# Keeping TensorE in source order through the scan stages of a hybrid decoder, and moving one pair of gate columns

## The chip, the cores and the metric

The kernel runs on one core of a Trainium2 chip. A core has TensorE (PE: matrix products, with its weight loads shown apart as PEld), VectorE (DVE), ScalarE (ACT), GpSimd (POOL) and SyncE (SP); each works through its own queue in order, and semaphores connect them. Transfers are issued from SP's and POOL's queues. The metric is the device time of one execution in microseconds (us).

## The reference, cut to what matters

One decoder layer is computed for 256 prompt positions and for 8 samples of 4 positions, 288 columns in all, so one weight pass serves both. The part that matters here is the mixer: two recurrent branches, merged by gates.

```python
xn = _rmsnorm(x, p['norm_mix'])
z, xbc, dt_raw, q, k, v, r, g_lr, gate_a, gate_b = _split(xn @ p['w_in'], IN_SIZES)
xbc, ssd_conv_new = _causal_dwconv(xbc, ssd_conv, p['ssd_conv_w'], p['ssd_conv_b'])
xs, Bm, Cm = _split(jax.nn.silu(xbc), ...)
y_ssd, ssd_state_new = _ssd_scan(xs_h, dt, A, Bm, Cm, ssd_state)      # 4 groups of 8 heads
u = (y_ssd + D * xs_h) * silu(z)
u = u * rsqrt(mean(u * u per group) + EPS) * ssd_norm
branch_a = u @ p['w_ssd_out']
...
o, gla_state_new = _gla_scan(qh, kh, vh, glog, gla_state)             # 4 heads
branch_b = (normalised o * silu(r)) @ p['w_gla_out']
merged = sigmoid(gate_a) * branch_a + sigmoid(gate_b) * branch_b
h = x + merged @ p['w_mix_out']
```

Cross-attention, the ConvFFN and the projections of the memory follow or precede it and are untouched.

## The kernel before, in words

**Main work.** Every large product is a projection (`proj_w`): two column tiles of 128 are accumulated over the depth. Weights come as `raw` tiles of 512 KB on SP's queue (3 buffers), and are split in two steps into a high part (`whi`, ACT, L103) and a low part (`wlo`, DVE, L105), 5 buffers each. Each half tile (two depth steps of 128) gives 12 matmuls of 288 columns: four each at L147 and L148 with the high part, four at L151 with the low part. After a half tile the generator yields. A projection of depth 16 has 8 half tiles, one of depth 4 has 2. When a projection is done, `cons` takes its two accumulators out of PSUM; accumulators have two tags with two buffers, used in turn.

**Scan work.** Between the half tiles stands the work of a scan: `ssd_scan` for the four SSD groups, then `gla_scan` for the four GLA heads. It is a generator too. In an SSD scan these PE steps come in order: products and transpositions of B, C and x (L755 to L763); the chunk's state products (L790 to L796); the products with the decay matrices (L837 to L841) and a transposition of the samples' x (L845); eight state updates (L907); the samples' product with their states (L886, with L889); the transposition back (L942); and in `finish` the sum of squares over the group (L972), which DVE and ACT prepare as a high and a low part (`sqh`, `sql`). The sample states are loaded on POOL's queue (L746, L734) and transposed on DVE (L900).

**Stages.** There are eight, n = 0 to 7. In stage n the scan of unit n runs as background, and `weave` pulls it so many steps for so many half tiles of main work (`N_BG[n]` steps in `N_MAIN[n]`). Main work is the projection of unit n+1, and, from n = 1, the output projection of unit n-1 (`project`) behind its first 16 half tiles. In stage 0, which has no such projection, the first half of the gate columns (`gate` with `gate_early`: 4 projections of 8 half tiles, called pairs of column tiles here) stands behind it instead. Their tanh is taken on ACT (L1231) and stored to DRAM on POOL's queue (L1233); it is read again in `project(3)` (`branch_a`), which runs in stage 4.

**Caches of the convolution.** The x, B and C columns pass through a short convolution on ACT, DVE and POOL (`conv_silu`); POOL copies the rows to keep into a cache tile (L638, L639). The cache is transposed on PE (L616). That step is put on a list (`late`), and `flush` runs it inside the next projection, behind its third half tile (its second in a projection of depth 4).

**Order.** The whole kernel is planned: `tc.block(schedule_with_timeline_sim=True)` simulates the engines and may issue an instruction ahead of an earlier one of the same engine that is not ready in the simulation. `tc.manual_schedule(engines=...)` takes the engines it names out of this: their instructions stay in the order in which the code gives them. It is used before for the first memory projection alone.

Of the kernel before, what the change touches and what calls it, by code (L numbers as in the profile page):

```python
# [27 lines left out]
O_Z, O_XBC, O_DT, O_Q, O_K, O_V, O_R, O_G, O_GA, O_GB = (  # L28
    0, 2048, 5120, 5152, 6176, 7200, 9248, 11296, 11312, 13360)
# [5 lines left out]
WB = 5  # L35
STOP = object()
LNEXP = "natural_log_exp_and_others"
N_MAIN = [64, 64, 48, 64, 64, 64, 64, 45]
N_BG = [60] * 4 + [44] * 3 + [47]


# [1 line left out]
def hybrid_step(ctx: ExitStack, tc: tile.TileContext, I: dict, O: list):  # L43
# [22 lines left out]
    def mm_tile():  # L66
        return ps.tile([P, 512], F32, tag="mm", bufs=3, name="mm")
# [96 lines left out]
    def proj(w, c0, ncol, X, nk, cons, row0=0):  # L164
        def load(k0, kn):
            return wload(rows_of(w, row0, k0, kn, c0, ncol))
        return proj_w(load, ncol, X, nk, cons)

    def run(*gens):
        for g in gens:  # L170
            for _ in g:
                pass

    def chain(*gens):
        for g in gens:
            yield from g

    def weave(main, bg, n_main, n_bg):

        done = 0  # L180
        for i, _ in enumerate(main):
            while done < (i + 1) * n_bg // n_main:
                w = next(bg, STOP)
                if w is STOP:
                    break
                done += 1 if w is None else w
        run(bg)

    def split_from(hi, lo, src, scale):
        S.activation(hi, src, ACT.Identity, scale=scale)  # L190
        V.scalar_tensor_tensor(lo, src, scale, hi, ALU.mult, ALU.subtract)

    def split(hi, lo, src):
        S.copy(hi, src)
        V.tensor_tensor(lo, src, hi, ALU.subtract)
# [10 lines left out]
    def bigf(name):  # L206
        return big.tile([P, KT, T], F32, tag="bigf", bufs=1, name=name)
# [15 lines left out]
    def rstd_from(pl, ssq, n, four=False):  # L223
        r = pl.tile([P, T], F32, tag="rstd", bufs=1, name="rstd")
        S.activation(r, ssq, ACT.Ln, scale=1.0 / n, bias=epsc[:, 1:2] if four else epsc[:, 0:1])
        S.activation(r, r, ACT.Exp, scale=-0.5)
        return r
# [351 lines left out]
    def b2r(name):  # L579
        return pa.tile([P, 512], F32R, tag="b2", bufs=10, name=name)  # L580
# [131 lines left out]
    def ssd_scan(g, xsT, sz):  # L712
# [245 lines left out]
        yield  # L958
        yield
        yield from finish(sz, acc, vec("ssd_norm")[:, 4 * g:4 * g + 4], True)  # L960

    fin = []

    def finish(u, sq, gcol, four):

        if len(fin) < 7:
            sp = b2r("sqh")[:, 0:T], b2r("sql")[:, 0:T]
            split(*sp, sq)
            yield
            ssq = mm_tile()  # L970
            for w in range(2):
                MM(ssq[:, 0:T], ones.bitcast(F32R), sp[w], start=(w == 0), stop=(w == 1))  # L972
        else:
            ssq = mm_tile()
            MM(ssq[:, 0:T], ones, sq, start=True, stop=True)
        rstd = rstd_from(pa, ssq[:, 0:T], 512, four)
        yield
        un = pa.tile([P, 8, T], F32R, tag="un", bufs=1, name="un")
        for t in range(4):
            V.tensor_tensor(u[:, t, :], u[:, t, :], rstd, ALU.mult)  # L980
            split_from(un[:, t, :], un[:, 4 + t, :], u[:, t, :], gcol[:, t:t + 1])
            if t % 2:
                yield
        fin.append(un)

    def out_proj(w, g, u, dst, post=None):
        for j2 in range(KT // 2):
            def cons(j, a, j2=j2):
                t = 2 * j2 + j
                if g == 0:  # L990
                    S.copy(dst[:, t, :], a)
                else:
                    V.tensor_tensor(dst[:, t, :], a, dst[:, t, :], ALU.add)
                if post:
                    post(t)
            yield from proj(w, 256 * j2, 256, two(u, 4), 4, cons, row0=512 * g)
# [71 lines left out]
    def gla_scan(h, eb, qe, ke, kd, kde, vT, sr, vd):  # L1068
# [145 lines left out]
        yield  # L1214
        yield
        yield from finish(sr, sq, rg, False)

    def gate(o, cons_t, j0=0, j1=KT // 2):
        for j2 in range(j0, j1):
            def cons(j, a, j2=j2):  # L1220
                cons_t(2 * j2 + j, a)
            yield from proj(I["w_in"], o + 256 * j2, 256, X, KT, cons)

    gq = []
    GH = KT // 4
# [41 lines left out]
    def start(n):  # L1267
        kind, i = units[n]
        got = []
        outs[n] = got  # L1270
        return ssd_proj(i, got) if kind == "s" else gla_proj(i, got)

    def project(n):

        kind, i = units[n]
        dst = ma if kind == "s" else mb
        yield from out_proj(I["w_ssd_out"] if kind == "s" else I["w_gla_out"], i, fin[n], dst, branch_a if n == 3 else None)

    def steps(g, n):
        for _ in range(n):  # L1280
            if next(g, STOP) is STOP:
                return
            yield

    run(start(0))
    for n in range(8):
        kind, i = units[n]
        scan = (ssd_scan if kind == "s" else gla_scan)(i, *outs[n][0])
        nxt = start(n + 1) if n < 7 else gate(O_GA, gate_a, GH)
        if n == 5:  # L1290
            mb = bigf("mb")
        parts = [nxt, gate(O_GA, gate_early, 0, GH)] if n == 0 else [steps(nxt, 16), project(n - 1), nxt]
        weave(chain(*parts), scan, N_MAIN[n], N_BG[n])
    run(project(7))
    pa_cm.__exit__(None, None, None)
    p1_cm.__exit__(None, None, None)
# [602 lines left out]
```

## Time and profile before

| | |
|---|---|
| median of 3 runs | 2500.24 us (2498.2 to 2500.59) |
| the profiled execution | 2500.31 us |
| its span, first to last instruction | 2498.6 us |
| busy: PE / PEld / DVE / ACT / POOL | 99% / 96% / 71% / 53% / 18% |
| SSD scans, beginning of the first to the end of the fourth | about 255 to 714 us |
| GLA scans | about 714 to 1156 us |

In a row of a timeline stand the start, the duration, the engine, the line, the operation, what it writes and reads, and how many were merged; in brackets the idle time before it and what ended that. A row of the waits gives the total in us, how often, and the longest. A row of the groups gives the count behind an x, then busy time and mean ns of one, then the engine's idle time before. PEclk is the granted clock of TensorE, 1.00 being full. Matmuls are pipelined, so two neighbours overlap in the rows.

### The profile page before, as it was taken

The numbers are of one execution on the slowest core, as the hardware profiler recorded it, in microseconds if no ns is written. First come the engines' busy times: TensorE is split into PE (matmuls) and PEld (weight loads), VectorE is DVE, ScalarE is ACT, GpSimd is POOL, SyncE is SP. The second block draws the span as 40 slices with busy tenths as digits, with TensorE's granted clock in tenths as the row PEclk, the third lists the DMA queues.
The fourth block names the chain that finished last, engine by engine and source line by source line (L and its number), as shares of the span: only waits on it lengthen the run. The fifth ranks groups of instructions, "written<-read, shape, count | busy, mean of one in ns | idle before, by whom it ended". The sixth has DMA issues, their size and how long they took to land.

```text
span 2498.6 us, 50407 instructions
## 1 busy us (share of the span) xinstructions
PE 2480.6 (99%) x18794; PEld 2398.5 (96%) x18794; DVE 1769.2 (71%) x3788; ACT 1332.1 (53%) x2717; POOL 445.3 (18%) x792
## 2 busy tenths in 40 slices
PE   9999999999999999999999999999999999999998
PEld 8889999999999999999999989999999999999998
DVE  6756777797877666777666577667777677675766
ACT  6656647656464655544444545555555454454545
POOL 3102133342311010110111122402111011020012
PEclk9999999999999999999999999999999999999999
DMA  8776587777869686877778599655555555555556
GB/s 246 250 226 203 165 250 203 238 203 221 256 207 290 191 266 188 250 227 237 214 228 271 186 329 334 196 163 173 171 170 171 171 170 172 169 172 170 169 172 171
DMA packets 445302, 528.51 MB, mean 212 GB/s; under 512 B 28492, under 2 KB 391852, under 8 KB 445024
## 3 DMA queue, kind: packets, MB, share of 16 engines
q1 hardware_dynamic: 408512, 422.35, 55.3%
q0 software_dynamic: 36512, 102.93, 12.8%
q8 instruction: 147, 2.41, 0.4%
q14 instruction: 99, 0.81, 0.1%
q10 hardware_dynamic: 32, 0.01, 0.0%
HBM read 476.41 MB, written 48.76 MB: 210 GB/s over the span
## 4 chain that ended last, share of the span: by engine, by line
PE 97%; DMA 1%; DVE 1%; ACT 0%; issue 0%; SPq 0%; DVEq 0%; ACTq 0%
PE acc L148 28%; PE acc L147 27%; PE acc L151 27%; PE acc L321 2%; PE acc L325 2%; PE acc L322 2%; PE mm L1195 1%; PE la L1186 1%; PE la L1529 1%; PE la L1586 1%; DMA raw<-in_w_cq_dram 0%; PE mm L1155 0%; DMA raw<-in_w_in_dram 0%; DMA mt<-in_mem_prompt_dram 0%; PE la L886 0%; PE mm L1169 0%
## 5 line engine op out<-in xcount | busy, mean ns | idle before, releaser
L103 ACT CAST whi<-raw 128x512 fp32r<-128x512 f32 x1464 | 894.0, 617 | 1014.7 <-PE acc L148 728.9
L105 DVE TENSOR_TENSOR wlo<-raw,whi 128x512 fp32r<-128x512 f32 x1464 | 996.2, 688 | 590.7 <-ACT whi L103 577.2
L147 PE MATMUL acc<-xn,whi 128*128 128x288 f32 (+1 forms) x1936 | 540.8, 295 | 3.1 <-DVE sz L652 2.2
L148 PE MATMUL acc<-xn,whi 128*128 128x288 f32 (+1 forms) x1936 | 541.5, 296 | 0.0
L151 PE MATMUL acc<-xn,wlo 128*128 128x288 f32 (+1 forms) x1936 | 409.5, 294 | 0.5 <-DVE wlo L105 0.5
L148 PE MATMUL acc<-hf,whi 128*128 128x288 f32 x1408 | 393.1, 296 | 0.0
L147 PE MATMUL acc<-hf,whi 128*128 128x288 f32 x1408 | 389.0, 292 | 0.0
L147 PEld LDWEIGHTS acc<-xn,whi 128*128 128x128 f32 (+1 forms) x1936 | 363.6, 188 | 8.1 <-ACT whi L103 2.8
L148 PEld LDWEIGHTS acc<-xn,whi 128*128 128x128 f32 (+1 forms) x1936 | 364.1, 188 | 4.4 <-issue 1.5
L151 PEld LDWEIGHTS acc<-xn,wlo 128*128 128x128 f32 (+1 forms) x1936 | 310.4, 188 | 2.2 <-issue 1.1
L151 PE MATMUL acc<-hf,wlo 128*128 128x288 f32 x1408 | 294.6, 290 | 0.0
L148 PEld LDWEIGHTS acc<-hf,whi 128*128 128x128 f32 x1408 | 264.6, 188 | 0.1
L147 PEld LDWEIGHTS acc<-hf,whi 128*128 128x128 f32 x1408 | 264.0, 188 | 0.1
L151 PEld LDWEIGHTS acc<-hf,wlo 128*128 128x128 f32 x1408 | 226.2, 188 | 0.0
L148 PE MATMUL acc<-pr,whi 128*128 128x288 f32 x704 | 196.6, 296 | 0.0
L147 PE MATMUL acc<-pr,whi 128*128 128x288 f32 x704 | 194.7, 293 | 0.0
L1700 POOL COPY fsp<-fst 128x16 f32<-128x16 f32 x88 | 38.8, 444 | 651.9 <-DVE av L1712 430.7
L151 PE MATMUL acc<-pr,wlo 128*128 128x288 f32 x704 | 147.3, 290 | 0.0
L147 PE MATMUL acc<-un,whi 128*128 128x288 f32 x512 | 143.1, 295 | 0.1
L148 PE MATMUL acc<-un,whi 128*128 128x288 f32 x512 | 143.1, 295 | 0.0
L148 PEld LDWEIGHTS acc<-pr,whi 128*128 128x128 f32 x704 | 132.3, 188 | 0.0
L147 PEld LDWEIGHTS acc<-pr,whi 128*128 128x128 f32 x704 | 132.0, 188 | 0.0
(529 smaller groups left out, 4322.8 us busy)
## 6 DMA issues: line engine op xcount, KB each, us to landing
raw<-in_w_in_dram SPq DMA_DIRECT2D x240, 512.0 KB
raw<-in_w_up_dram SPq DMA_DIRECT2D x176, 512.0 KB
raw<-in_w_down_dram SPq DMA_DIRECT2D x88, 512.0 KB
raw<-in_w_cv_dram SPq DMA_DIRECT2D x32, 512.0 KB
raw<-in_w_ssd_out_dram SPq DMA_DIRECT2D x32, 512.0 KB
sin<-in_state_gla_dram POOLq DMA_DIRECT2D x32, 512.0 KB, 6.6
out_dram<-sin SPq DMA_DIRECT2D x32, 512.0 KB
raw<-in_w_gla_out_dram SPq DMA_DIRECT2D x32, 512.0 KB
```

Source lines behind the costliest of these rows:

```text
L103: S.copy(hi, raw)
L105: V.tensor_tensor(lo, raw, hi, ALU.subtract)
L147: MM(a, hi[:, k, cs], xh, start=(k0 + s0 + k == 0), stop=False)
L148: MM(a, hi[:, k, cs], xl, start=False, stop=False)
L151: MM(a, lo[:, k, cs], xh, start=False, stop=(k0 + s0 + k == nk - 1))
L321: MM(accs[m], mn_hi[:, kk, ms_], hi[:, 0, :], start=(kk == 0), stop=False)
L322: MM(accs[m], mn_lo[:, kk, ms_], hi[:, 0, :], start=False, stop=False)
L325: MM(accs[m], mn_hi[:, kk, ms_], lo[:, 0, :], start=False, stop=(kk == KT - 1))
L1186: MM(osa[NS * j:NS * j + NS, :], qdm[:, k, b, :], sins[b][:, k, :], start=False, stop=(q == 1 and k == 0))
L1195: MM(a, kb[:, k * P:(k + 1) * P], vst, start=True, stop=True)
L1529: MM(ssc[NS * c:NS * c + NS, 0:P], xq[:, j, u, :], kt[:, j], start=(j == 0), stop=(j == 15))
L1700: G.tensor_copy(sp[:, :, 0:2], st.rearrange("p (b k) -> p b k", k=2))
```

## The change

Three things are done together. PE's instructions of the eight scan stages stay in source order. The last of the four early gate pairs goes from the end of stage 0 to the end of stage 2, and the pace of both stages is set anew: 60 background steps in 56 half tiles in each, where it was 60 in 64 and 60 in 48. And in `finish` the sum of squares stands one background step later, in SSD scans two.

```diff
-N_MAIN = [64, 64, 48, 64, 64, 64, 64, 45]
+N_MAIN = [56, 64, 56, 64, 64, 64, 64, 45]
 N_BG = [60] * 4 + [44] * 3 + [47]
...
             sp = b2r("sqh")[:, 0:T], b2r("sql")[:, 0:T]
             split(*sp, sq)
             yield
+            yield
+            if four:
+                yield
             ssq = mm_tile()
...
-        parts = [nxt, gate(O_GA, gate_early, 0, GH)] if n == 0 else [steps(nxt, 16), project(n - 1), nxt]
-        weave(chain(*parts), scan, N_MAIN[n], N_BG[n])
+        parts = [nxt, gate(O_GA, gate_early, 0, GH - 1)] if n == 0 else [steps(nxt, 16), project(n - 1), nxt]
+        if n == 2:
+            parts.append(gate(O_GA, gate_early, GH - 1, GH))
+        with tc.manual_schedule(engines={mybir.EngineType.PE}):
+            weave(chain(*parts), scan, N_MAIN[n], N_BG[n])
```

## The prediction

> **What bounds the kernel now.** I read the page first: its busy line, then the chain that ended last.
>
> ```profile
> PE 2480.6 (99%) x18794; PEld 2398.5 (96%) x18794; DVE 1769.2 (71%) x3788; ACT 1332.1 (53%) x2717; POOL 445.3 (18%) x792
> ...
> PE 97%; DMA 1%; DVE 1%; ACT 0%; issue 0%; SPq 0%; DVEq 0%; ACTq 0%
> ```
>
> PE is busy 99% and carries 97% of the chain: the end moves only when PE idles, runs at a lower clock, or gets other work. The change gives it no other work, so only idle time and clock can move. Busy time by stage comes next: first to fourth SSD scan (second to fifth row follow the heading), then the four GLA scans together. Columns: length, then busy time of PE, PEld, DVE, ACT, POOL, then the granted clock, DMA share and GB/s.
>
> ```profile
> core 0: us, PE busy (x) PEld busy (x) DVE busy (x) ACT busy (x) POOL busy (x), PEclk, DMA share, GB/s
> 255.00:379.00 124.00, 124.00 (x970) 120.75 (x969) 91.95 (x191) 63.79 (x131) 37.07 (x64) 1.00 0.74 213
> 379.00:497.00 118.00, 118.00 (x923) 114.73 (x922) 92.03 (x194) 77.55 (x179) 39.16 (x72) 1.00 0.76 224
> 497.00:610.00 113.00, 109.90 (x844) 105.83 (x844) 91.48 (x202) 62.85 (x137) 46.23 (x68) 0.99 0.79 227
> 610.00:714.00 104.00, 103.89 (x797) 99.68 (x796) 87.18 (x195) 58.24 (x106) 27.57 (x43) 0.99 0.71 204
> 714.00:1156.00 442.00, 442.00 (x3320) 423.81 (x3319) 311.37 (x621) 224.50 (x408) 49.65 (x76) 1.00 0.76 239
> ```
>
> Of 901 us only the third SSD stage loses PE time, 3.1 us, and the clock dips with it. PE's waits over 250 to 1160 us:
>
> ```profile
> PE acc L147 <- DVE sz L652: 2.2, 1, 2.2
> PE acc L147 <- ACT whi L103: 0.9, 1, 0.9
> ```
>
> The two instructions that stood behind them, in the timeline (the idle time is in brackets):
>
> ```profile
> 563.85 0.40 PE L147 MATMUL acc<-xn,whi 128*128 128x288 f32 x1 [0.94 <-ACT whi L103]
> ...
> 606.42 0.40 PE L147 MATMUL acc<-xn,whi 128*128 128x288 f32 x1 [2.16 <-DVE sz L652]
> ```
>
> And the 20 us around the longer one, columns as in the stages above:
>
> ```profile
> 600.00:610.00 10.00, 7.84 (x54) 7.61 (x53) 6.28 (x14) 6.66 (x16) 0.00 (x0) 0.90 0.46 143
> 610.00:620.00 10.00, 10.00 (x75) 10.00 (x75) 8.27 (x19) 7.06 (x14) 0.00 (x0) 0.93 0.12 37
> ```
>
> All that can be won here is 0.94 + 2.16 of idle time, and the clock that the second one cost: (1 - 0.90) x 10 + (1 - 0.93) x 10 = 1.7 us. Together 4.8 us, or 0.19% of the execution's 2500.31 us. That is the ceiling of the gain.
>
> **How far the planner's order is from source order.** This decides what pinning PE does. Counting the yields in the code, the state multiplication (L886) stands 29 half tiles of main work behind the last sample transposition (L845) at the pace of 60 background steps in 64 main ones, and 21 at the third stage's 60 in 48. A half tile has four L147 instructions, so the trace's distance is the count below, by four, in scans one to four:
>
> ```profile
> 313.70:361.36 47.66, 32.11 (x116) 21.76 (x116) 1.00 0.92 270
> 427.45:475.35 47.90, 32.15 (x116) 21.77 (x116) 1.00 0.88 261
> 534.20:593.84 59.64, 39.67 (x143) 26.84 (x143) 1.00 0.96 273
> 636.58:686.07 49.49, 32.41 (x116) 21.81 (x116) 1.00 0.88 258
> ```
>
> 29, 29, 35.75 and 29. In three scans the planner already runs PE in source order there, without a wait; in the third it put the step about 15 half tiles (24 us) later than the source. So pinning is mostly no change, and is a real one in the third stage, around it, and in the second scan (below).
>
> **The change part by part.**
>
> Pair moved. It is 8 half tiles, with 8 casts, 8 subtractions, 4 weight loads on SP's queue, 2 tanh and 1 store on POOL's queue:
>
> ```profile
> L103 ACT CAST whi<-raw 128x512 fp32r<-128x512 f32 x1464 | 894.0, 617 | 1014.7 <-PE acc L148 728.9
> L105 DVE TENSOR_TENSOR wlo<-raw,whi 128x512 fp32r<-128x512 f32 x1464 | 996.2, 688 | 590.7 <-ACT whi L103 577.2
> ```
>
> The gate's own tanh and store (duration in ns as least, median, most):
>
> ```profile
> L1231 ACT ACTIVATE gq<-acc x8: 397/404/412, 344.2 to 386.9; 128x288 f32<-128x288 f32 x8
> L1233 POOL DMA_DIRECT2D ga_d<-gq x4: 565/572/578, 347.9 to 387.6; - x4
> ```
>
> A half tile of main work takes (47.66 us - about 2.4 of scan work) / 29 = 1.56 us, so the pair takes 12.5 us of PE in either place: zero net. It costs DVE only 8 x 0.688 = 5.5 us and ACT 8 x 0.617 + 2 x 0.40 = 5.7 us in those 12.5, so it thins the stage it joins and thickens the one it leaves. Third stage: DVE (91.5 + 5.5) / (113 + 12.5) = 77% against 81%. First: (92.0 - 5.5) / (124 - 12.5) = 78% against 74%, which is what the second stage has now (92.0 / 118 = 78%) without an idle PE. The cover of the first stage holds, as far as averages tell. The POOL store (0.57 us) now stands in the third stage, before the fourth scan's loads, which are not urgent then. The value is read back in the project behind the fourth scan, so nobody waits for it.
>
> Pace. The third scan is spread over 60 in 56 instead of 60 in 48, and the pair comes last in its main work. There the gated projection needs no DVE operation on its accumulator, only a tanh. The 2.16 us were a projection waiting for the DVE consumer of an accumulator queued behind the scan's squares; that consumer now has 12.5 us more. The 0.94 us were weights late while DMA ran at 0.96 of its capacity (third row of the four); 4 x 512 KB in 12.5 us is 168 GB/s, under the 273 there. I take both as gone with the clock loss: -4.8 us.
>
> Later sum of squares (L972). In the trace the planner already pulls main matmuls between the two halves:
>
> ```profile
> 824.74 0.29 PE L972 MATMUL mm<-sqh,ones 128*128 128x288 f32 x1
> ...
> 825.52 0.29 PE L972 MATMUL mm<-sql,ones 128*128 128x288 f32 x1
> ```
>
> Pinned without the extra yields, each of seven would wait up to 0.8 us (5.5 in all); one or two half tiles more (1.6 to 3.1 us) cover that. The normalised result is wanted by the project 16 half tiles (25 us) into the next stage, so later costs nothing. Zero.
>
> Pinned PE. What is now behind a late instruction is every later matmul. The place where the trace shows this clearly is the second scan. The transposition of the B/C convolution cache (L616) stands in source one half tile behind L886/L889. PE was there at 479.3; the cache was not:
>
> ```profile
> 475.35 1.92 PE L886 MATMUL la<-st,cdm 128*32 128x512 f32 x16
> ...
> 479.30 0.29 PE L147 MATMUL acc<-xn,whi 128*128 128x288 f32 x1
> ...
> 490.36 0.27 PE L616 MATMUL mm<-ident,cache 128*108 128x128 f32 x1
> ```
>
> The last accumulator of that convolution leaves PSUM on ACT here:
>
> ```profile
> 480.79 0.35 ACT L634 COPY cv<-acc 128x256 f32<-128x256 f32 x1
> ```
>
> And POOL, which writes the cache with L638 and L639, does this meanwhile:
>
> ```profile
> 478.59 2.14 POOL L728 DMA_DIRECT2D mab<-acum_d  x4 [1.40 <-ACT mss L865]
> 480.73 2.84 POOL L720 DMA_DIRECT2D ab<-acum_d  x4
> ...
> 484.13 0.20 POOL L639 COPY cache<-cv 128x24 f32<-128x24 f32 x1
> ```
>
> ACT frees the last accumulator from 480.79 on, POOL is held by eight transfer issues until 483.6, and the copies end at 484.3. At its source place L616 would wait 5.0 us. Were POOL free, the copies would end by about 481.8 (ACT's copies, then two short ones): 2.5 us. If the new plan brings the convolution forward it is zero. Ends 0 and 5.0; I take 2.5, since ACT's row has to come first in any order of POOL. An idle stretch of that length is nearest to the 2.16 that cost 1.7 us of clock, so 1.7 comes with it: +4.2. In return the second scan's tail, now held until 490, runs early and unloads the start of the third stage; that is what makes the -4.8 safe.
>
> [...]
>
> Sum, on the profiled execution's 2500.31 us (median of the runs 2500.24, so the same): 2500.3 - 4.8 + 0 + 0 + 4.2 = 2499.7 us.
>
> **Rivals.**
> 1. No new wait: the cache is ready by its place. 2500.3 - 4.8 = 2495.5. For it: the other five L616 and all L886 of three scans stand at source place without a wait. Against: the rows above.
> 2. The wait at L616 is there but the clock holds: 2500.3 - 4.8 + 2.5 = 2498.0. Against it: the 0.90 row. For it: a wait of 0.94 us cost no clock. [...]
> 3. Slower: in the third scan the pinned L886 waits for the sample states. Its source place is now 25 half tiles behind L845, at 534.2 + 25 x 1.56 + 2 = 575 us on this trace's scale.
>
> ```profile
> 566.06 1.44 POOL L746 DMA_DIRECT2D sqr<-in_state_ssd_dram  x2 [0.38 <-DMA sqr<-in_state_ssd_dram]
> ```
>
> That is POOL's last issue of states for this scan. The landing times of all of them in that stage, and DVE's last transposition:
>
> ```profile
> DMA to landing us min/median/max: 2.2/5.6/7.7
> ```
>
> ```profile
> 590.05 0.70 DVE L900 STREAM_TRANSPOSE st<-sqr 128x512 f32<-128x512 f32 x1
> ```
>
> The last states were issued by 567 and landed around 572.5, in time by 2.5 us; but DVE turned the last one only at 590.75. If DVE keeps that order PE waits up to 15.7 us, with the clock 17.4: 2500.3 - 4.8 + 17.4 = 2512.9. If DVE turns them as they land it is zero. With half the wait, 7.9 + 1.7, the time is 2505.1, the point where it counts as slower. Against it: the stage's DMA and DVE load fall with the slower pace, and the other three scans are in place. Its middle, with L616's 4.2 before it, is about 2508.
> 4. Nothing moves: the planner's stall comes back elsewhere (the first stage, now at the same pace): 2500.3.
>
> **How the numbers follow.** Forecast 0.38 (own range 2497 to 2502.5, the latter with L616 at its full 5.0), rival 1 0.28, rival 2 0.08, rival 3 0.18, rival 4 0.08. The range 2494.8 to 2508 leaves out the better part of a gain with extras below and the upper half of rival 3. The change is measurable from about 0.2% (5 us), so under 2495.3 is faster, over 2505.3 slower. Rival 1 lies on that edge: 0.17 of its 0.28, with a little from the others, makes 0.2 faster; rival 3 and some of the forecast's tail make 0.23 slower; 0.57 are within.
>
> **What would show it.** Right: no idle PE on a DVE consumer of sz at the end of the third scan, clock 1.00 there; PE's waits list L616 on POOL's cache copy (2 to 5 us) and the clock dips behind it; L886 of the third scan 25 half tiles (100 L147) behind L845; GLA stages as before. Wrong: a wait of PE on the DVE transposition of states, on a split weight (wlo) in the first or third stage, or L616 without a wait.

## The result, and the profile after

The changed kernel takes 2523.90 us (median; 2522.36 to 2529.38) against 2499.22 us before: 1.0095 times as long, 95% interval [1.0079, 1.0111], or some 24 us. Measured once more beside other kernels it was 1.0083 [1.0069, 1.0096]. The prediction had 2499.7 us, in a range that ended at 2508: the kernel is 16 us above that end.

The page of the changed kernel, its busy line and its chain:

```profile
PE 2489.7 (98%) x18794; PEld 2402.2 (95%) x18794; DVE 1770.3 (70%) x3788; ACT 1335.2 (53%) x2717; POOL 439.1 (17%) x792
...
PE 87%; DMA 7%; DVE 2%; issue 1%; POOL 1%; ACT 1%; SPq 0%; DVEq 0%; ACTq 0%; POOLq 0%
```

Matmuls and instructions are as many as before. The chain has changed: PE carried 97% of it and carries 87%, and 7% are transfers. The stages, from one scan's first products to the next's (columns as in the prediction; a scan's work stands at other places of the main work than before, so the rows are read by themselves and not subtracted):

```profile
255.00:384.00 129.00, 126.49 (x987) 123.17 (x985) 95.67 (x202) 70.25 (x147) 37.26 (x64) 1.00 0.73 208
384.00:505.00 121.00, 115.79 (x882) 112.08 (x881) 92.53 (x199) 78.40 (x181) 39.29 (x72) 0.97 0.71 206
505.00:616.00 111.00, 106.04 (x810) 100.63 (x809) 87.65 (x193) 53.03 (x109) 34.96 (x60) 0.98 0.74 205
616.00:733.00 117.00, 114.81 (x894) 111.13 (x893) 91.13 (x199) 66.24 (x127) 33.26 (x51) 1.00 0.76 218
733.00:1180.00 447.00, 442.05 (x3286) 421.77 (x3285) 308.17 (x615) 223.37 (x406) 49.81 (x76) 0.99 0.74 235
```

Before, one stage lost 3.1 us of PE; now each loses: 2.5, 5.2, 5.0, 2.2 and 5.0 (length less PE's busy time). The profiled execution took 2529.38 us, 5.5 above its median, so the account is made on the second profile of the same kernel (2521.69 us). PE's waits there from 250 to 1180 us:

```profile
PE la L886 <- DVE st L900: 6.4, 2, 3.9
PE mm L616 <- POOL cache L639: 4.6, 1, 4.6
PE la L1189 <- DMA sin<-in_state_gla_dram: 2.6, 2, 1.4
PE acc L147 <- DVE ma L996: 1.8, 2, 1.2
PE mm L1098 <- DVE qe L1057: 1.1, 2, 0.7
```

And the stretches of 10 us with a lower clock (the eighth column is PEclk):

```profile
350.00:360.00 10.00, 7.49 (x47) 4.51 (x47) 5.47 (x15) 2.02 (x5) 1.75 (x4) 0.83 0.68 195
470.00:480.00 10.00, 5.39 (x29) 5.16 (x28) 5.41 (x14) 5.54 (x17) 5.43 (x11) 0.70 0.66 211
480.00:490.00 10.00, 10.00 (x74) 10.00 (x74) 6.08 (x13) 8.92 (x24) 0.00 (x0) 0.96 0.13 29
580.00:590.00 10.00, 7.24 (x44) 4.22 (x45) 4.91 (x10) 2.15 (x7) 3.30 (x5) 0.83 0.78 222
1090.00:1100.00 10.00, 10.00 (x69) 10.00 (x70) 8.66 (x25) 3.47 (x8) 0.57 (x1) 0.83 0.58 175
```

Waits: 6.4 + 4.6 + 2.6 + 1.8 + 1.1 = 16.5 us. Clock (the share that is missing, times the 10 us): 1.7 + 3.0 + 0.4 + 1.7 + 1.7 = 8.5 us. Part of this second sum is in the first already, because the clock fell to half before the wait on L616 was over; in this stretch PE is idle (no busy time) and the clock is 0.50:

```profile
473.98:476.39 2.41, 0.00 (x0) 0.00 (x1) 1.72 (x5) 0.46 (x1) 2.36 (x6) 0.50 0.93 271
```

So 2.41 x 0.5 = 1.2 us of the clock's loss cost nothing more, and 7.3 us remain. Gone are the two stalls of before with their clock, 4.8. That makes 16.5 + 7.3 - 4.8 = 19.0 us; the two profiled executions differ by 2521.69 - 2500.31 = 21.4. Most of the time went into these five waits and the clock behind them; 2.4 us are not accounted for.

### The profile page after: what moved, and what is told of

The parts are those of the page before. It is cut to its first block, busy times and chain, and to the rows that moved or that the text cites. A ratio compares the mean times of both kernels' runs of the same rounds, so it can differ in the third digit from the quotient of the medians.

```text
span 2527.7 us, 50401 instructions
## 1 busy us (share of the span) xinstructions
PE 2489.7 (98%) x18794; PEld 2402.2 (95%) x18794; DVE 1770.3 (70%) x3788; ACT 1335.2 (53%) x2717; POOL 439.1 (17%) x792
## 3 DMA queue, kind: packets, MB, share of 16 engines
q8 instruction: 147, 2.41, 0.4%
## 4 chain that ended last, share of the span: by engine, by line
PE 87%; DMA 7%; DVE 2%; issue 1%; POOL 1%; ACT 1%; SPq 0%; DVEq 0%; ACTq 0%; POOLq 0%
PE acc L148 26%; PE acc L147 25%; PE acc L151 25%; PE acc L321 2%; PE acc L322 2%; PE acc L325 2%; DMA raw<-in_w_cq_dram 1%; DMA kc<-in_cache_mem_k_dram 1%; DMA raw<-in_w_cv_dram 1%; DMA raw<-in_w_in_dram 1%; DVE wlo L105 1%; PE la L1189 1%; DMA sin<-in_state_gla_dram 1%; PE mm L1198 1%; PE la L1535 1%
## 5 line engine op out<-in xcount | busy, mean ns | idle before, releaser
L103 ACT CAST whi<-raw 128x512 fp32r<-128x512 f32 x1464 | 895.1, 618 | 1023.6 <-PE acc L148 738.7
L105 DVE TENSOR_TENSOR wlo<-raw,whi 128x512 fp32r<-128x512 f32 x1464 | 994.6, 687 | 590.8 <-ACT whi L103 580.9
L147 PE MATMUL acc<-xn,whi 128*128 128x288 f32 (+1 forms) x1936 | 543.5, 296 | 0.6 <-ACT ma L994 0.6
L147 PE MATMUL acc<-hf,whi 128*128 128x288 f32 x1408 | 389.0, 292 | 0.0
L147 PEld LDWEIGHTS acc<-xn,whi 128*128 128x128 f32 (+1 forms) x1936 | 365.0, 189 | 7.0 <-issue 5.4
L147 PEld LDWEIGHTS acc<-hf,whi 128*128 128x128 f32 x1408 | 264.0, 188 | 0.1
L147 PE MATMUL acc<-pr,whi 128*128 128x288 f32 x704 | 194.7, 293 | 0.0
L147 PE MATMUL acc<-un,whi 128*128 128x288 f32 x512 | 143.8, 296 | 2.3 <-DVE ma L996 2.2
L147 PEld LDWEIGHTS acc<-pr,whi 128*128 128x128 f32 x704 | 132.0, 188 | 0.0
```

The source lines that it names most:

```text
L103: S.copy(hi, raw)
L105: V.tensor_tensor(lo, raw, hi, ALU.subtract)
L147: MM(a, hi[:, k, cs], xh, start=(k0 + s0 + k == 0), stop=False)
```

## The experiments

Costs below are (ratio - 1) x 2500 us. A 95% interval reaches 2 to 4 us to either side, so a difference of 3 us between two kernels is not clear of noise. The waits are those of one profiled execution each.

**Pin and pair apart.** Three kernels do one part alone.

```diff
 # the change without its pin
-        with tc.manual_schedule(engines={mybir.EngineType.PE}):
-            weave(chain(*parts), scan, N_MAIN[n], N_BG[n])
+        weave(chain(*parts), scan, N_MAIN[n], N_BG[n])
 # pin and later sum of squares alone: also N_MAIN and parts of the kernel before
 # later sum of squares alone: only the yields in finish
```

> The change without its pin: the pair in stage 2, both paces and the later sum of squares stay, PE is planned again. Theory A (the time was lost in waits at the head of a PE queue that may no longer pull later work ahead): the moved pair does what the prediction gave it, so about 2499.2 - 4.8 = 2494.4 us (2492 to 2497), no wait on L616 nor on L900, and clock 1.00 through the SSD stages. Rival B (the pair and the paces make the new waits, because sample states come due earlier in the first scan and the third stage is longer): 2510 us or more, with waits on L900 still in the list. Between, 2497 to 2502: the planner's two stalls have come back in another place, and the change had no gain to lose.

> The pin and the later sum of squares alone: pair and paces as in the kernel before. Theory A: L616 waits about 4.8 us with about 3.4 of clock, the last GLA stage loses about 8.5 us, the first scan's L886 (2.7) does not wait, but the third scan's L886 stands only 21 half tiles behind L845 and so about 6 us earlier than in the changed kernel, so it waits about 4.9 + 6 us; in all 2499.2 + 8.2 + 8.5 + 10.9 + 1.7 + about 2 = 2530 us (2520 to 2538). Rival B: without the new paces no wait on L900 of more than 1 us; 2510 to 2517 us.

> The later sum of squares alone: pair, paces and PE's planning as in the kernel before. The prediction's step 4: nothing, 2500 us (2498 to 2502). Rival: the shifted step alone makes the planner lay PE's order of the third stage anew and the late weights hit another place, 2503 us or more with other waits than 0.9 and 2.2 us between 530 and 650 us; then the 7 us of the planned kernel with the pair are not the pair's.

| kernel | median, us | ratio, 95% | cost, us |
|---|---|---|---|
| later sum of squares alone | 2500.98 | 1.0004 [0.9996, 1.0013] | 1.0 |
| change without its pin | 2507.13 | 1.0025 [1.0015, 1.0035] | 6.3 |
| pin and later sum alone | 2522.31 | 1.0085 [1.0071, 1.0099] | 21.3 |
| the change | 2523.90, again 2522.40 | 1.0095, again 1.0083 | 23.8, 20.8 |

The later sum of squares is free. The pin, with it, costs all that the change costs. The pair and its paces, planned, cost 6.3 us by themselves and, within the intervals, nothing on top of the pin. Both theories failed on the pair: it gave no 4.8 us, but it made no wait on L900 either. On the pin theory A has the time (2520 to 2538), but not the wait: the third scan's L886 waits 2.7 us and not some 11, and L907 ahead of it 3.8. The two stalls of the kernel before are gone in the pinned kernel without the pair as well (0.4 us on L103 is left), so the pair and the paces are not needed for that.

**The pin stage by stage.** Pair and paces as before, PE pinned in one part only; and the change with its last stage planned.

```diff
+        with tc.manual_schedule(engines={mybir.EngineType.PE}) if n == 1 else ExitStack():
 # likewise n == 2; n > 3; and in the changed kernel n < 7
```

> Pair and paces as before, the later sum of squares in, and PE kept in source order in the second stage (n = 1) alone. The prediction gave this +4.2 us on L616. Theory G (each stage's pin has its own price, which can be added up): the 4.8 us wait on L616 as in all pinned kernels, and 1.7 to 3.4 us of clock: 2500.8 + 7.4 = 2508.2 us (2506 to 2510). Rival (the price depends on what the next stage does: planned again, it takes the time back or adds to it): 2504 us or less, or 2512 or more.

> As before with PE in source order in the third stage (n = 2) alone, at its old pace of 60 in 48. Theory G: waits on L907 (4.0 us) and L886 (2.8 us) and 1.7 us of clock as with all stages pinned, and the two stalls of the kernel before (4.8 us with their clock) gone: 2500.8 + 8.5 - 4.8 = 2504.5 us (2502.5 to 2507). Rival (the pin costs nothing there and wins the ceiling): 2497 us or less; the other rival (the stall comes in the next stage, on the project's accumulators): over 2508 us with a wait on L996 between 630 and 665 us.

> As before with PE in source order in the four GLA stages alone (n = 4 to 7). Theory G: nothing in the first three but about 0.8 us for a state (L1189), and in the last about 1.4 us on L1098, 1.5 to 3.4 on L1189 and 1.7 of clock: 2500.8 + 6.5 = 2507 us (2505 to 2509.5). The prediction said 0. Rival (these waits come only because the SSD stages before ran late): within 2 us of the kernel before.

> The changed kernel with PE planned again in the last GLA stage alone (n = 7). Theory A: the waits of L1098 and L1189 in that stage (about 1.4 and 3.4 us) and the clock lost behind them (2 x 1.7) come back: 2523.9 - 8.2 = 2515.7 us (2513.5 to 2518). Rival C (the sample states of the last scan are late whatever the order, and PE would wait at another instruction): 2521 us or more, with a wait for sin or kc in that stage. In the stages before nothing differs.

The second stage alone: ratio 1.0024 [1.0015, 1.0033], 6.0 us. The third alone: 1.0046 [1.0033, 1.0060], 11.5. The GLA stages alone: 1.0026 [1.0015, 1.0036], 6.5; their profiled execution was the fastest of theirs, 2503.81 us against a median of 2508.85, so its waits show the lower end. Their sum, 24.0, is near the 21.3 of all eight; the first and the fourth stage were not pinned alone. The waits of the second, the third and the GLA stages, each from the kernel that pins it:

```profile
PE mm L616 <- POOL cache L639: 4.2, 1, 4.2
```

```profile
PE mm L907 <- DVE sin L910: 4.3, 1, 4.3
PE la L886 <- DVE st L900: 3.2, 1, 3.2
PE acc L147 <- DVE ma L996: 1.4, 2, 1.0
PE mm L763 <- ACT rstd L225: 1.2, 1, 1.2
```

```profile
PE la L1189 <- DMA sin<-in_state_gla_dram: 4.0, 2, 3.0
...
PE mm L1098 <- DVE qe L1057: 0.7, 1, 0.7
```

So the price is spread over the stages, and the prediction had looked at one of them. Theory G has the second stage and the GLA stages, and misses the third (2502.5 to 2507 us expected, 2513.56 measured): the waits shown are 10.1 us instead of 6.8, with L996 in the next stage and L763 besides the two that it named, and the clock lost 3.4 instead of 1.7. The other rival, which had a wait on L996 and over 2508 us, holds. The changed kernel with its last stage planned took 2517.57 us, 1.0066 [1.0053, 1.0079]: 5.7 us less than the mean of the two measurements of the change and within theory A's 2513.5 to 2518. The wait of L1189 is not the same in each execution: 3.2 us at most in the first profile of the changed kernel, 1.4 in the second.

**Taking single waits away.**

```diff
 # cache transposition 8 half tiles later (ssd_proj)
-            late.append(lambda cache=cache: conv_cache(cache, D + 128 * g, D + 512 + 128 * g))
+            bc_cache = cache
...
+            if g % 2 == 0 and j2 == 0:
+                late.append(lambda cache=bc_cache: conv_cache(cache, D + 128 * g, D + 512 + 128 * g))
 # samples' product three steps later in scans one and three
+        if g % 2 == 0:
+            yield 3
         inter()
```

Lines behind an insertion have higher numbers in these kernels: L996 of the changed kernel is L998 in the second, and L815 and L955 are L817 and L957 in the first.

> The changed kernel with the transposition of the B/C convolution cache (L616) put 8 half tiles later in source, into the second projection of sz. Theory A: its wait of 4.8 us and the 3.4 us of clock behind it go, nothing else moves: 2523.9 - 8.2 = 2515.7 us (2513 to 2518.5), clock 1.00 from 470 to 490 us. Rival D (the wait only hides another one: with PE running on, the next scan's first products or the project behind it become late by the same time): 2520 us or more, with a new wait of 2 us or more between 470 and 510 us.

> The changed kernel with the samples' product (L886) three background steps later in source in the first and the third scan. Theory A (PE's place in its queue is the whole cost): its waits of 2.7 and 4.9 us and the 1.7 us of clock go: 2523.9 - 9.3 = 2514.6 us (2512 to 2517.5). Theory E (the weights themselves are late there: in the third scan ScalarE waits 4.7 us for a weight load up to 582.9, VectorE's next low part stands behind that cast and the transposition of the states behind that): PE takes one more half tile and then waits at 582 to 584 us for the weights; the third scan gives back 3 us at most, the first its 2.7: 2518 to 2522 us, with a wait of 1.5 us or more on L103 or L105 between 575 and 592 us.

> The changed kernel with all three mends: the last GLA stage planned, the cache transposition 8 half tiles later, the samples' product of scans one and three later. Singly they gave 6.3, 1.2 and 5.5 us. If the prices add up: 2523 - 13 = 2510 us (2507.5 to 2512.5). Rival (each wait that is taken away is taken up by the next one): 2515 us or more. If their waits go in full, as theory A had it, 2523 - 25.7 = 2497 us.

The cache kernel took 2522.68 us, 1.0089 [1.0075, 1.0103]: nothing gained. Its L616 does not wait, but 12 us later in the same stage a projection does, on an accumulator that ScalarE and VectorE had not emptied:

```profile
490.39 0.61 PE L147 MATMUL acc<-xn,whi 128*128 128x288 f32 x1 [5.34 <-DVE sz L652]
```

What stood ahead is seen in ScalarE's queue of that kernel. The decay work of the next scan (L817) was planned ahead of the activation that reads the accumulator (L651), with squares of the scan (L957) and casts of weights between them:

```profile
481.06 2.44 ACT L817 ACTIVATE m<-ab,tokc 128x128 f32<-128x128 f32 x8
...
489.05 0.43 ACT L957 ACTIVATE th<-sz 128x288 f32<-128x288 f32 x1
489.39 0.69 ACT L651 ACTIVATE th<-acc 128x288 f32<-128x288 f32 x2
```

Rival D holds: in place of the wait on L616 stands another of about the same length. The later product of the samples gave 2518.45 us, 1.0077 [1.0065, 1.0089], some 3 us less than the change where theory A had 9.3, and that is not clear of noise. Its two waits were still 5.0 us in all (6.4 and 7.3 in the two profiles of the change) though L886 stands about three half tiles later, so the transpositions came later too, and 3.5 us on the add of the project (L996 of the changed kernel) came up in the fourth stage. Theory A falls with these waits; theory E's time holds, but its wait on L103 or L105 did not show. All three mends together: 2512.87 us, 1.0048 [1.0036, 1.0061], about 10 us less than the change and 12 more than before. The single gains (5.7, nothing and 3) add up about; the 25.7 us of the full waits do not come back. A wait of 4.3 us on the accumulator of sz and 3.0 us on the project's add are left.

**Late weights.** Why is the transposition of the states late in the third scan? In the changed kernel POOL had issued the last of the states that it waits for by 565.2 us, and no load of a square tile (L746) in that stage took over 6.6 us to land. VectorE turned the last one only at 585.4, and PE stood behind it:

```profile
564.60 0.65 POOL L746 DMA_DIRECT2D sqr<-in_state_ssd_dram  x1 [1.26 <-DMA sqr<-in_state_ssd_dram]
```

```profile
582.91 1.14 ACT L103 CAST whi<-raw 128x512 fp32r<-128x512 f32 x2 [4.71 <-DMA raw<-in_w_in_dram]
```

```profile
583.56 0.69 DVE L105 TENSOR_TENSOR wlo<-raw,whi 128x512 fp32r<-128x512 f32 x1 [1.78 <-ACT whi L103]
...
585.37 0.70 DVE L900 STREAM_TRANSPOSE st<-sqr 128x512 f32<-128x512 f32 x1
```

```profile
586.12 2.75 PE L886 MATMUL la<-st,cdm 128*32 128x512 f32 x12 [4.75 <-DVE st L900]
```

A weight load is late, ScalarE's cast waits 4.71 us for it, VectorE's next low part waits for the cast, and the transposition stands behind that low part in VectorE's queue. Two kernels leave out 2 MB of transfers there, the stores of the third scan's updated sample states; what they leave out is part of the result.

```diff
-                if t % 2:
+                if t % 2 and g != 2:
                     for b in range(4):
```

> The changed kernel without the stores of the updated sample states of the third SSD scan (16 transfers of 128 KB from SP's queue, L915; that output stays empty). Theory E (the transfers of that stage are at their limit, DMA share 0.9 to 1.1 from 540 to 590 us, and weights land late): without these 2 MB the weights land in time, L886 of the third scan waits under 1 us, and with it the clock holds: 2523.9 - 6.6 = 2517.3 us (2515 to 2519.5), L886 of the first scan still waits 2.7. Theory A (order alone): the wait of 4.9 us at L886 stays and the time is within 2 us of the changed kernel's.

> The change without its pin, and without the stores of the updated sample states of the third SSD scan (16 transfers of 128 KB from SP's queue; that output stays empty). Theory E: the waits of 5.3 us (L907, 547 us) and 2.3 us (634 us) of the unpinned kernel were late weights; the first goes with its clock (3.4 us), so 2507.1 - 8.7 = 2498.4 us or less (2494 to 2500.5). Rival F (they come from the planner's order, whatever the transfers do): 2505 us or more, with a wait over 4 us between 535 and 600 us.

Pinned: 2519.85 us, 1.0080 [1.0067, 1.0094]. ScalarE no longer waits for a load between 570 and 585 us. The third scan's wait, 4.8 and 3.9 us in the two profiles of the change, is 1.9 here (4.7 less the first scan's 2.8), not under 1 as theory E had it. The clock lost less, about 3.4 us by an estimate that takes all else as equal: the waits from 250 to 1180 us are 17.4 us against 16.5 in the second profile of the change, and the profiled execution took 2519.14 us against 2521.69. The waits on L886 here:

```profile
PE la L886 <- DVE st L900: 4.7, 2, 2.8
```

So late weights are about half of that wait. For the rest the trace shows other work in VectorE's queue, which no run takes away: in this kernel VectorE has no idle time from 577.12 to 581.25 us, with four updates of states (L910) and these two low parts ahead of the last transposition, while the loads of its states had been issued by 562 us:

```profile
579.34 1.29 DVE L105 TENSOR_TENSOR wlo<-raw,whi 128x512 fp32r<-128x512 f32 x2
580.55 0.70 DVE L900 STREAM_TRANSPOSE st<-sqr 128x512 f32<-128x512 f32 x1
```

The first scan's wait looks the same: in the changed kernel its last states were issued by 337 us, and VectorE is busy for 6.46 of the 6.53 us from 349.36 to 355.89, with updates and low parts ahead of the last two transpositions. PE's order was fixed; the order of VectorE, ScalarE and POOL was still the planner's. In time the gain is 2.3 us, within the two intervals. Unpinned: 2506.63 us, 1.0023 [1.0015, 1.0032], as with the stores. The first wait halves (5.3 to 2.6 us), and the fourth stage waits 3.6 us on L996 where it had waited 2.3 (for L1006, at the same project) and 0.8. Rival F has the time and theory E the shrinking of the first wait: less traffic moved the loss to the next place.

**Pace, and where the project meets the states.** The next two ask whether the pair's place or the pace costs the 6.3 us; then the fourth stage's wait is taken up.

```diff
 # from the change without its pin
-N_MAIN = [56, 64, 56, 64, 64, 64, 64, 45]
+N_MAIN = [56, 64, 48, 64, 64, 64, 64, 45]    # or 52
 # project earlier: from the kernel with 48, and from the change
+... [steps(nxt, 8 if n == 3 else 16), project(n - 1), nxt]
```

> PE planned, the pair in the third stage, but the third scan at its old pace of 60 steps in 48 half tiles, so that the pair stands behind its tail. Theory H (the slower pace is at fault: at 60 in 56 the loads of the sample states start about 17 half tiles into the stage, just when the project's weights come, instead of 15): no wait over 1.5 us between 535 and 600 us, and the stall of 2.2 us on sz at the stage's end is gone: 2496 us (2494 to 2499.5). Rival (the pair's place is at fault): 2504 us or more, with a wait over 2 us between 535 and 665 us.

> As the one before, with 60 steps in 52 half tiles. Theory H: between the two, 2497 to 2504 us. Rival (the planner's order decides by chance of its simulated times, no pace is better than another in order): outside of that, or the wait in another place than 535 to 560 us.

Old pace: 2506.22 us, 1.0020 [1.0010, 1.0031]. Pace 52: 2509.28, 1.0034 [1.0021, 1.0046]. Theory H falls: with the old pace the third stage still waits 2.5 us, 1.7 of it on sz (L652), the stall that was to be gone, and the fourth stage loses 4.2 us; pace 52 (2497 to 2504 us expected) misses too. The rival, that the pair's place is at fault, has the time and a wait in its window, but it does not say why that wait comes:

```profile
PE acc L147 <- DVE ma L996: 4.2, 1, 4.2
PE acc L147 <- DVE sz L652: 1.7, 1, 1.7
PE mm L907 <- ACT cst L618: 0.8, 1, 0.8
```

What is late there is an addition of the project (L996), in VectorE's queue behind a row of scan operations that runs without idle time from 635.3 us on; ahead of them VectorE had waited 2.88 us for the cast of a late weight (old pace):

```profile
631.57 1.14 ACT L103 CAST whi<-raw 128x512 fp32r<-128x512 f32 x2 [3.81 <-DMA raw<-in_w_ssd_out_dram]
```

```profile
632.23 1.29 DVE L105 TENSOR_TENSOR wlo<-raw,whi 128x512 fp32r<-128x512 f32 x2 [2.88 <-ACT whi L103]
...
640.25 2.48 DVE L900 STREAM_TRANSPOSE st<-sqr 128x512 f32<-128x512 f32 x4
...
643.59 0.78 DVE L996 TENSOR_TENSOR ma<-acc,ma 128x288 f32<-128x288 f32 x2
```

```profile
644.15 0.58 PE L147 MATMUL acc<-un,whi 128*128 128x288 f32 x1 [4.23 <-DVE ma L996]
```

In the kernel before, the project of that stage began at 618.74 and the second burst of state loads was issued at 633.25, 14.5 us behind it:

```profile
618.74 0.43 PE L147 MATMUL acc<-un,whi 128*128 128x288 f32 x2
```

```profile
633.25 3.16 POOL L734 DMA_DIRECT2D sin<-in_state_ssd_dram  x4 [0.77 <-DMA sqr<-in_state_ssd_dram]
```

In the kernel with the old pace it was the other way round, 624.41 and 619.98:

```profile
624.41 0.29 PE L147 MATMUL acc<-un,whi 128*128 128x288 f32 x1
```

```profile
619.98 2.99 POOL L734 DMA_DIRECT2D sin<-in_state_ssd_dram  x4 [0.88 <-DMA sqr<-in_state_ssd_dram]
```

The runs divide by this. In the kernel before, with the later sum alone, and with the pin in the second or in the GLA stages alone the states come 14 to 15 us behind the project's first matmul, and no L996 waits there. Wherever the third stage is pinned or holds the pair they come 3 to 6 us ahead of it, and in each of those PE waits for some accumulator during the project (the longest of these waits is 1.0 to 4.2 us). Two kernels move the project alone.

> The planned kernel with the pair in the third stage and the third scan's old pace, and the output projection of the third scan 8 half tiles earlier in the fourth stage (behind 8 half tiles of the next projection instead of 16). Theory K (in the fourth stage the loads of the sample states and the weights of that projection collide; in the kernel before the projection began 14.5 us ahead of the states, here 4.4 us behind them): the states come about 8 us behind its beginning, the 4.2 us wait on L996 shrinks under 1.5 us and the clock holds: 2506.2 - 5 = 2501 us (2497 to 2503). Rival L (the adds into ma are late because VectorE has too much to do there, whatever the transfers): the wait stays over 2.5 us and the time within 2.5 us of 2506.

> The changed kernel with the same projection 8 half tiles earlier in the fourth stage. Theory K: its two waits of 0.8 and 1.4 us on L996 go: 2523 - 2.2 = 2521 us (2518 to 2523); the loads of the states begin 3 us or more behind the projection's first matmul. Rival L: the waits stay; or, with PE pinned, a new wait on the normalised result (un) at the head of the projection, 2524 us or more.

Planned: the states come 8 us behind the project, the wait on L996 falls from 4.2 to 0.9 us as theory K has it, and the time stays: 2506.65 us, 1.0029 [1.0018, 1.0039]. The project is now too early for its own input, and the 10 us from 620 us ran at a clock of 0.83:

```profile
619.11 0.40 PE L148 MATMUL acc<-un,whi 128*128 128x288 f32 x1 [1.98 <-DVE un L191]
```

Pinned: 2521.47 us, 1.0087 [1.0074, 1.0101]; L996 waits 1.0 instead of 1.8 us, too little to show in the time. So theory K has the wait and not the time. Even for that one wait the collision of transfers is not shown as the cause: an earlier project also takes most of its adds (L996) out of VectorE's queue behind the scan's row, and the 0.9 us that are left stand behind that row again, five transpositions (L900) up to 649.5 us.

**The change again**, whose profile the account above uses:

> The changed kernel once more, beside the single pins: 2523.9 us (2522 to 2526). Its waits of 4.8 us on L616, 4.9 us on L886 of the third scan and 2.7 us on L886 of the first should stand again to within 0.7 us; the wait for a GLA state near 1149 us, which was 1.2 to 3.4 us in the pinned kernels, should differ from 3.4, and the 2.5 us in the projections of the memory ahead of the scans should be smaller, as in the other kernels with the same code there.

2522.40 us. L616 (4.6 us in both) and the first scan's L886 (2.5) stand to 0.1 us between the two profiles, the third's waits 3.9 instead of 4.8, the last GLA stage's state 1.4 instead of 3.2, and the wait for casts ahead of the scans shrank from 2.5 to 0.7 us. None of the kernels ran faster than the one before.

## Why the prediction was wrong

Right, by its own steps:
- **PE bounds and only idle time and clock can move.** The account above closes within 2.4 us on these two alone.
- **The places in source order.** L886 of the third scan stands 100 L147 behind L845, as counted:

```profile
538.47:586.10 47.63, 28.17 (x100) 18.78 (x100) 1.00 1.00 274
```

- **Later L972.** Zero: 1.0004 [0.9996, 1.0013].
- **L616's mechanism.** POOL was held by eight issues and the copies came behind them, in the changed kernel too:

```profile
472.56 2.15 POOL L728 DMA_DIRECT2D mab<-acum_d  x4 [1.40 <-ACT mss L865]
474.71 2.85 POOL L720 DMA_DIRECT2D ab<-acum_d  x4
...
477.82 0.20 POOL L639 COPY cache<-cv 128x24 f32<-128x24 f32 x1
```

Wrong, in the order of size:
- **"The place where the trace shows this clearly is the second scan."** This step gave the pin its term in the sum, +4.2 us, from one stage; the pin measured 21.3 us (with the later sum, which is free). In the second stage the term is near: 6.0 us, interval 3.8 to 8.3. Put at nothing without a price were the others: the third stage costs 11.5 us and the GLA stages 6.5 when pinned by themselves. That scans one, two and four already stood in source order at L886 without a wait was read as "pinning is mostly no change"; but pinned kernels wait at other places too (L907, L763, L1098, L1189, the project), where the planned order of before had no wait, and these were not looked at. "GLA stages as before" was wrong for the first (0.7 to 1.2 us on L1189 in the changed kernel) and the last.
- **Rival 3** had the mechanism (L886 waits for the transposition L900) at 0.18. In the third scan it waited 4.8 us of the 15.7 allowed, and 3.9 in the second profile; what made the time 2524 was that it came together with the waits of the other stages; the prediction added only L616's 4.2 to it (and came to "about 2508" where its own terms give 2509.3). Its remark that the other three scans are in place fell too: the first scan's L886 waits 2.5 us at its new pace, and not at all in the kernel that is pinned at the old one.
- **L616 at 2.5 us and 1.7 of clock.** It took 4.6 us, near the full end of 5.0, and 2.2 of clock: 6.8 us at half clock, 2.4 of them within the wait. The value between the ends rested on POOL being free, and nothing in the change frees POOL. Taking that wait away gives nothing, as the next one is as long.
- **Pair and pace, -4.8.** The two stalls did go. But the pair with its paces, planned, costs 6.3 us instead, and pinned they win nothing that the pin had not already taken away. The 1.7 us of clock in the 4.8 were of one execution (see the last section). The DVE share of the third stage was averaged over it, and the DMA share was taken to fall with the pace; in the planned kernel weights came late in the third stage, where PE waited 5.3 us at L907 for a copy (L618) that stood on ScalarE behind casts which had waited 5.06 and 1.70 us for their weights, and in the fourth:

```profile
549.39 1.14 ACT L103 CAST whi<-raw 128x512 fp32r<-128x512 f32 x2 [5.06 <-DMA raw<-in_w_in_dram]
```

```profile
553.07 0.79 PE L907 MATMUL mm<-bblk,wst 128*128 128x512 f32 x1 [5.30 <-ACT cst L618]
```

  Rival 4 (the planner's stall comes back elsewhere) was nearest, and too small.

What stays open: why the planner no longer begins the fourth stage's project ahead of the states once the pair stands in the third, whether the transfers or VectorE's queue make its adds late, and what would have to move so that both that wait and the one on `un` are gone. A project 12 half tiles into the stage instead of 8 or 16 has no run. The first and the fourth stage's pin were not priced alone.

## What to carry to other kernels

A planned order without waits does not say that source order has none: PE did not wait at L616, L907 and L886 in the kernel before, and waited 4.6, 3.8 and 2.7 us there with the pin and the later sum alone. The price of pinning a queue was the lateness of the inputs that the plan had stepped around, and each pinned stage had to be priced at each of its places. A wait that was taken away was worth no more than its distance to the next one behind it: 4.6 us on L616 went, 5.34 us on sz came, and the time was 2522.68 us. Fixing one engine's order beside engines whose order is still planned left it to wait for what the plan put last on the others, as L616 did for POOL's copies behind eight issues of 5.0 us. And the busy share of a stage, of VectorE or of the transfers, says nothing of the few microseconds in which an input is due (VectorE is busy 74% of the changed kernel's first stage, and 6.46 of the 6.53 us ahead of its last transpositions); there the queue of the engine that makes it has to be read.

## What the hardware showed beyond that

The clock. PE idle for 2.51 us ahead of the same instruction in two executions of the same kernel: once the 10 us around it ran at a clock of 1.00 and once at 0.83. The two rows of the timeline, and the first one's stretch (the second's stands above):

```profile
355.94 1.92 PE L886 MATMUL la<-st,cdm 128*32 128x512 f32 x16 [2.51 <-DVE st L900]
```

```profile
353.66 2.85 PE L886 MATMUL la<-st,cdm 128*32 128x512 f32 x16 [2.51 <-DVE st L900]
```

```profile
350.00:360.00 10.00, 7.49 (x59) 5.59 (x58) 7.52 (x20) 2.42 (x7) 1.34 (x3) 1.00 0.91 267
```

The same holds of the stall that the prediction counted on: 2.16 us on sz were followed by 0.90 and 0.93 in the kernel before, and by 1.00 in the kernel with the GLA stages pinned. Two waits of 1.1 us in all on L1098 were followed by 0.83 at 1090 us in the second profile, and by 1.00 in the changed kernel without the stores. So the clock's loss is not a function of the wait's length alone: behind waits of 1 to 5 us these profiles show no half clock, 3.4 us of it or 6.8 (a loss of 0, 1.7 or 3.4 us, less what falls into the wait). The stretch at 0.50 in the kernel before, behind the 2.16 us on sz:

```profile
607.90:611.25 3.35, 3.35 (x16) 3.35 (x16) 0.00 (x0) 0.00 (x0) 0.00 (x0) 0.50 0.00 0
```

And three in the first profile of the changed kernel, at 4.63 us on L616 (the last 1.0 us of that wait is in it), behind 4.75 us on the third scan's L886, and behind 0.32 and 0.73 us on L1098:

```profile
477.00:483.80 6.80, 5.73 (x24) 5.73 (x25) 1.72 (x5) 4.70 (x15) 1.02 (x4) 0.50 0.58 205
586.20:589.60 3.40, 3.40 (x18) 0.81 (x20) 0.00 (x0) 0.00 (x0) 2.60 (x4) 0.50 0.98 230
1094.80:1098.20 3.40, 3.40 (x18) 3.40 (x18) 3.39 (x13) 1.24 (x4) 0.35 (x1) 0.50 0.69 207
```

In the same profile two waits of 1.05 and 1.15 us on L996 were followed by 1.00 from 650 to 680 us. What decides between these outcomes is not shown here.
